# Logit tiles of two PSUM banks, read by one instruction each, in a two-layer hybrid attention kernel

## The chip, the cores and the metric

The kernel runs on one core of one Trainium2 chip. The metric is the device time of one execution in microseconds. Three executions of the kernel before took 3163.4 to 3169.52 us, median 3168.88. The profile shown here is of one more execution.

## The reference

One sequence of 2048 tokens, width 1024, two layers. Each layer projects the normalised state, runs four kinds of attention with four heads of 64 each, gates the joined result and adds the output product to the state:

```python
proj = jnp.einsum('bsd,dc->bsc', h_res, w_in[l])
(fq, fk, fv, f_logit, sq, sk, sv, c_q, c_kv, k_rot, mq, gate) = jnp.split(proj, offsets, axis=-1)
# fox: causal softmax of q.k*scale + f_cum[q] - f_cum[k]
# sb (stick-breaking): w = sigmoid(z) * prod over later valid keys of sigmoid(-z), no softmax
# mla: causal softmax, q and k built from RMS-normed latents c_q, c_kv plus a rope part
# mem: softmax over 256 memory keys
y = jnp.einsum('bsc,cd->bsd', mixed * jax.nn.silu(gate), w_out[l])
h_res = _layer_norm(DEEPNORM_ALPHA * h_res + y, ln_g[l], ln_b[l])
```

All inputs and outputs are float32. The kernel keeps float32 accuracy by splitting operands into a high and a low half in float16 and using three matmuls for one product (`mm3`).

## The kernel before

Work goes in stages, given by `PLAN`: the latents of a layer, then pairs of heads (fox0, fox1, mla0, mla1, sb0, sb1, and both mem pairs together), then the output product. A pair (`pair`) prepares its weights (`wprep`: load, maximum per partition, maximum over partitions in `allmax` through a PSUM tile named pm, scale, split into halves), then goes over four chunks of 512 tokens. For a chunk it makes k, q and v (tiles pk, pq, pv, 24 matmuls each), the gate (pg, `gate_sig` for sb, `gate_tanh` for the others), and then per head and query tile of 128 rows the attention.

`scores` makes the logits of one query tile against up to 1024 keys, in parts of 512 columns, each in its own PSUM tile of one bank. `softmax_tile` (fox, mla) reads each part on DVE: it copies the logits to SBUF, for fox adding the forget sums fb, and takes their maximum (lines 369 and 371); line 376 joins the maxima; ACT then makes the exponentials (line 380). `stick_tile` (sb) reads each part twice on ACT, for sigmoid(-z) and sigmoid(z) (lines 398 and 399); DVE scans the first (401), POOL multiplies (402, 403). In both kinds the weights are split into halves (386, 387, 409, 410), transposed by DMA into tiles named pt, and multiplied with v (858). `half_sum` (449, 450) joins the halves of a head.

PSUM has eight banks. They are given out as four score slots, two slots for the outputs o and two for projections:

```python
ps_s = pool("ps_s", 4, bass.MemoryType.PSUM)
ps_o = pool("ps_o", 2, bass.MemoryType.PSUM)
ps_p = pool("ps_p", 2, bass.MemoryType.PSUM)
```

Score slots also hold the gate (pg), the latent blocks of a layer (pl, read at 537 to 541) and the transposed forget logits (pf, 587), the k and v products of mem, and the tiles of the output product (936, read at 940). Projection slots hold pk, pq, pv, pr and pm. Within a pool slots are handed out in the program's order: a tile takes the slot of the tile before it by the number of slots, once that is free.

The order on each engine is set by a scheduler that goes through the program with a timeline of its own and takes what is ready there, by program order as priority; scores of fox rank 60 places earlier (`SCORE_AHEAD`). Each engine then runs its list in order, and so do the DMA queues: nearly every transfer is issued by SP, in the order of its list. After the latents, `forget` makes running sums of the forget logits, which return through DRAM as fb.

## Time and profile before

| | us |
|---|---|
| median of three executions | 3168.88 |
| lowest, highest | 3163.4, 3169.52 |
| the profiled execution, its own time | 3167.7 |
| span of its profile | 3165.9 |
| PE, DVE, ACT, POOL busy | 2560.0, 2432.3, 1913.7, 1268.3 |
| mean granted TensorE clock | 0.915 of full speed |

Busy time is the union of an engine's instructions. The profile of an instruction runs from its start to the end of its writes; on DVE and ACT the next one starts before that, so the distance of two starts, not the duration, is what an instruction costs in a dense row. An idle stretch of an engine is put down to the instruction whose end released what came next.

### The profile page before, as it was taken

The numbers are of one execution on the slowest core, as the hardware profiler recorded it, in microseconds if no ns is written. First come the engines' busy times: TensorE is split into PE (matmuls) and PEld (weight loads), VectorE is DVE, ScalarE is ACT, GpSimd is POOL, SyncE is SP. The second block draws the span as 40 slices with busy tenths as digits, with TensorE's granted clock in tenths as the row PEclk, the third lists the DMA queues.
The fourth block names the chain that finished last, engine by engine and source line by source line (L and its number), as shares of the span: only waits on it lengthen the run. The fifth ranks groups of instructions, "written<-read, shape, count | busy, mean of one in ns | idle before, by whom it ended". The sixth has DMA issues, their size and how long they took to land. (4 is left out here: it accounts for less than half of the span.)

```text
span 3165.9 us, 47289 instructions
## 1 busy us (share of the span) xinstructions
PE 2560.0 (81%) x16412; PEld 1374.7 (43%) x16412; DVE 2432.3 (77%) x4809; ACT 1913.7 (60%) x3543; POOL 1268.3 (40%) x871
## 2 busy tenths in 40 slices
PE   2589897888886785799978879978888768749898
PEld 2345454444553442444434545544445435325444
DVE  7857867888879989767655575689886998995675
ACT  3447657788757676465235565677776766755600
POOL 5303332333468786432210122233334877771300
PEclk9889899999997897899989999999999889869999
DMA  7747969889845745657845477798987575565652
GB/s 195 195 122 164 197 143 195 174 176 182 169 73 113 155 91 105 150 111 191 234 116 126 105 151 143 159 196 163 186 152 135 89 169 100 101 138 119 163 187 100
DMA packets 1225042, 469.49 MB, mean 148 GB/s; under 512 B 1040305, under 2 KB 1184945, under 8 KB 1224657
## 3 DMA queue, kind: packets, MB, share of 16 engines
q1 hardware_dynamic: 1224800, 466.46, 67.7%
q8 instruction: 129, 2.11, 0.3%
q14 instruction: 113, 0.92, 0.1%
HBM read 141.07 MB, written 50.53 MB: 61 GB/s over the span
## 5 line engine op out<-in xcount | busy, mean ns | idle before, releaser
L387 POOL TENSOR_TENSOR hl<-sb,hl 128x1024 f16<-128x1024 f32 (+2 forms) x192 | 325.0, 1694 | 878.4 <-ACT hl L386 718.5
L858 PE MATMUL o<-pt,v 128*128 128x256 f16 (+3 forms) x3456 | 436.5, 302 | 232.7 <-DMA pt<-hl 232.0
L332 PE MATMUL s<-k,q 128*128 128x512 f16 (+3 forms) x1920 | 523.3, 374 | 120.3 <-DVE sm L369 35.9
L403 POOL TENSOR_TENSOR sg<-sg,kp 128x127 f32<-128x127 f32 (+3 forms) x192 | 396.5, 2068 | 110.4 <-DVE kp L401 80.1
L858 PEld LDWEIGHTS <-v 128*64 128x64 f16 (+1 forms) x3456 | 247.1, 112 | 443.7 <-DMA pt<-hl 226.9
L380 ACT ACTIVATE sb<-sb,sm,sc_all 128x1024 f32<-128x1024 f32 (+7 forms) x384 | 377.4, 983 | 75.8 <-DVE sm L377 75.1
L386 ACT CAST hl<-sb 128x1024 f16<-128x1024 f32 (+7 forms) x384 | 298.4, 790 | 174.7 <-DMA pt<-hl 161.7
L936 PE MATMUL s<-wo,gc 128*128 128x512 f16 x1536 | 335.5, 381 | 2.3 <-DVE yt L940 2.1
L332 PEld LDWEIGHTS <-q 128*128 128x128 f16 x1920 | 184.5, 103 | 309.2 <-issue 193.8
L387 DVE TENSOR_TENSOR hl<-sb,hl 128x1024 f16<-128x1024 f32 (+2 forms) x192 | 208.3, 1085 | 76.4 <-ACT hl L386 75.6
L410 DVE TENSOR_TENSOR hl<-sg,hl 128x128 f16<-128x128 f32 (+3 forms) x192 | 240.5, 1259 | 32.8 <-ACT hl L409 31.7
L409 ACT CAST hl<-sg 128x128 f16<-128x128 f32 (+3 forms) x192 | 152.7, 798 | 178.5 <-DMA pt<-hl 89.4
L369 DVE CUSTOM_DVE_ANT_0 sb<-s,fb 128x512 f32<-128x512 f32 (+2 forms) x320 | 184.2, 604 | 80.9 <-DMA fb<-fds 39.7
L936 PEld LDWEIGHTS <-gc 128*128 128x128 f16 x1536 | 150.9, 98 | 184.5 <-issue 6.2
L398 ACT ACTIVATE kp<-s,sc_all 128x512 f32<-128x512 f32 (+2 forms) x320 | 200.3, 628 | 30.6 <-PE s L332 10.1
L401 DVE TENSOR_TENSOR_SCAN kp<-kp 128x384 f32<-128x384 f32 (+7 forms) x128 | 211.6, 1665 | 6.0 <-ACT kp L398 5.1
L399 ACT ACTIVATE sg<-s,sc_all 128x512 f32<-128x512 f32 (+2 forms) x320 | 200.1, 630 | 25.0 <-DVE hl L410 13.1
L276 PE MATMUL pv<-w,hT 128*128 128x128 f16 x1024 | 191.6, 227 | 18.7 <-DVE k L286 18.7
L276 PE MATMUL pg<-hT,w 128*128 128x512 f16 x512 | 199.8, 390 | 7.6 <-DVE sb L371 6.8
L277 PE MATMUL pg<-hT,w 128*128 128x512 f16 x512 | 199.5, 390 | 0.0
L278 PE MATMUL pg<-hT,w 128*128 128x512 f16 x512 | 198.8, 388 | 0.0
L454 POOL TENSOR_TENSOR og<-og,sg 128x512 f32<-128x512 f32 x64 | 96.4, 1507 | 251.0 <-DVE og L450 176.9
(240 smaller groups left out, 6072.3 us busy)
## 6 DMA issues: line engine op xcount, KB each, us to landing
raw<-in_w_in_dram SPq DMA_DIRECT2D x100, 256.0 KB, 3.6
q<-q SPq DMA_DIRECT2D x128, 128.0 KB, 2.5
fb<-fds SPq DMA_DIRECT2D x32, 512.0 KB, 4.3
gd<-gh SPq DMA_DIRECT2D x128, 128.0 KB, 2.5
raw<-in_w_out_dram SPq DMA_DIRECT2D x64, 256.0 KB, 4.2
gc<-gd SPq DMA_DIRECT2D x64, 256.0 KB, 5.2
yt<-ah SPq DMA_DIRECT2D x32, 512.0 KB, 5.1
raw<-ctd SPq DMA_DIRECT2D x48, 256.0 KB, 3.6
```

Of the source, the lines that this page charges most:

```text
L276: T.matmul(ps, lh, rh, start=(first and k == 0), stop=False)
L332: T.matmul(ps[:, :m], qs[:, h, v, j * P:(j + 1) * P], ks[c][:, h, :m], start=(v == 0), stop=last)
L380: A.activation(t, t, AF.Exp, scale=sc, bias=sm[:, 2:3], accum_out=su[:, b, col:col + 1])
L386: A.copy(hi, t)
L387: (G if j else V).tensor_tensor(lo, t, hi, op=ALU.subtract)
L398: A.activation(keep[:, o:o + m], ps[:, :m], AF.Sigmoid, scale=nsc)
L399: A.activation(w[:, o:o + m], ps[:, :m], AF.Sigmoid, scale=sc)
L401: V.tensor_tensor_scan(keep[:, ::-1], keep[:, ::-1], keep[:, ::-1], cy, op0=ALU.mult, op1=ALU.bypass)
L403: G.tensor_tensor(w[:, :n - 1], w[:, :n - 1], keep[:, 1:n], op=ALU.mult)
L410: V.tensor_tensor(lo, w, hi, op=ALU.subtract)
L858: T.matmul(o[r0:r1, oc + j0 * P:oc + 256], vs[k // 4][:, k % 4, h, 0:r1 - r0], pcol(pt, a, k % 8, kb, j0), start=(n == 1), stop=(n == total))
L936: T.matmul(ps, gc[a][k // 4][:, k % 4, t * P:(t + 1) * P], wo[k][:, b2, n * 512:(n + 1) * 512], start=(k == 0 and a == 0 and b2 == 0), sto ...
```

## The change

Score tiles become two banks wide (two slots of 1024 columns in the same four banks), and every reader takes the whole tile: one DVE read per block of up to 1024 keys in fox and mla, two ACT reads in sb. With up to two maxima left per query tile, their reduction becomes one operation on two numbers, and only where there are two blocks. The first 512 keys of two neighbouring query tiles share one tile (`duo`). The gate, the latent blocks, pf and mem's k and v products move to the projection slots. Mem's logits of a head take one tile instead of two, read by one maximum; the output product's two halves share one tile, read by one instruction.

```diff
-    ps_s = pool("ps_s", 4, bass.MemoryType.PSUM)
+    ps_s = pool("ps_s", 2, bass.MemoryType.PSUM)
...
     def s_tile():
-        return ps_s.tile([P, 512], F32, name=nm("s"), tag="s")
+        return ps_s.tile([P, 1024], F32, name=nm("s"), tag="s")
...
         npass = 3 if kind == "mla" else 2
-        parts = []
+        if n <= 512 and b == 0:
+            if j % 2 == 0:
+                duo[0] = s_tile()
+            full = duo[0][:, (j % 2) * 512:(j % 2) * 512 + n]
+        else:
+            full = s_tile()[:, :n]
         with tc.high_priority(offset=SCORE_AHEAD.get(kind, 0)):
             for o in range(0, n, 512):
                 c, m = 2 * b + o // 512, min(512, n - o)
-                ps = s_tile()
+                ps = full[:, o:o + m]
...
         for b in range(nb):
-            parts, n = scores(kind, h, i, b, qs, ks, qr, kr)
+            ps, n = scores(kind, h, i, b, qs, ks, qr, kr, duo)
             t = granule("sb")[:, :n]
-            for ps, o, m in parts:
-                mx = sm[:, 4 + np_:5 + np_]
-                np_ += 1
-                if kind == "fox":
-                    V.tensor_tensor_reduce(t[:, o:o + m], ps[:, :m], fb[b][:, o:o + m], 1.0, -3.0e38, ALU.add, ALU.max, mx)
-                else:
-                    V.tensor_scalar(t[:, o:o + m], ps[:, :m], 1.0, None, op0=ALU.mult, op1=ALU.max, accum_out=mx)
+            mx = sm[:, 4 + b:5 + b]
+            if kind == "fox":
+                V.tensor_tensor_reduce(t, ps, fb[b][:, :n], 1.0, -3.0e38, ALU.add, ALU.max, mx)
+            else:
+                V.tensor_scalar(t, ps, 1.0, None, op0=ALU.mult, op1=ALU.max, accum_out=mx)
             at.append(t)
         top = sm[:, 4:5]
-        if np_ > 1:
+        if nb > 1:
             top = sm[:, 0:1]
-            V.tensor_reduce(top, sm[:, 4:4 + np_], axis=AX.X, op=ALU.max)
+            V.tensor_tensor(top, sm[:, 4:5], sm[:, 5:6], op=ALU.max)
...
             keep, w = granule("kp")[:, :n], granule("sg")[:, :n]
-            for ps, o, m in parts:
-                A.activation(keep[:, o:o + m], ps[:, :m], AF.Sigmoid, scale=nsc)
-                A.activation(w[:, o:o + m], ps[:, :m], AF.Sigmoid, scale=sc)
+            A.activation(keep, ps, AF.Sigmoid, scale=nsc)
+            A.activation(w, ps, AF.Sigmoid, scale=sc)
...
-        ps = ps_s.tile([P, 512], F32, name=nm("pg"), tag="s")
+        ps = ps_p.tile([P, 512], F32, name=nm("pg"), tag="p")
...
-                    ps = ps_s.tile([P, 512], F32, name=nm("pl"), tag="s")
+                    ps = ps_p.tile([P, 512], F32, name=nm("pl"), tag="p")
...
-                pf = ps_s.tile([P, 512], F32, name=nm("pf"), tag="s")
+                pf = ps_p.tile([P, 512], F32, name=nm("pf"), tag="p")
...
-                ps = ps_s.tile([P, 512], F32, name=nm("pk"), tag="s")
+                ps = ps_p.tile([P, 512], F32, name=nm("pk"), tag="p")
...
-                        pss = [s_tile() for _ in range(2)]
+                        ps = s_tile()
...
-                        for u in range(2):
-                            psv = pss[u].rearrange("p (j k) -> p j k", j=2)
-                            V.tensor_reduce(sm[:, 2 * u:2 * u + 2], psv, axis=AX.X, op=ALU.max)
-                            V.tensor_scalar(sm[:, 4 + 2 * u:6 + 2 * u], sm[:, 2 * u:2 * u + 2], nsc, LN_TOP,
-                                            op0=ALU.mult, op1=ALU.add)
+                        psv = ps.rearrange("p (j k) -> p j k", j=4)
+                        V.tensor_reduce(sm[:, 0:4], psv, axis=AX.X, op=ALU.max)
+                        V.tensor_scalar(sm[:, 4:8], sm[:, 0:4], nsc, LN_TOP, op0=ALU.mult, op1=ALU.add)
...
+                    ps = s_tile()
                     for n in range(2):
-                        ps = s_tile()
...
-                        yv = yt[:, n * 512:(n + 1) * 512]
-                        V.scalar_tensor_tensor(yv, ps, u_o, yv, op0=ALU.mult, op1=ALU.add)
+                    V.scalar_tensor_tensor(yt, ps, u_o, yt, op0=ALU.mult, op1=ALU.add)
```

The scheduler orders the engines anew. Three places follow; in brackets stands the engine whose signal an instruction waits for, by the semaphore's name.

PE in layer 0, where the weight maxima of fox0 (pm_1453) stand. Before, they follow the second latent chunk's pf and the third chunk's first block (pl_1064):

```order
L278 MATMUL pl_888<-w_260,hT_380 128x420
L587 MATMUL pf_973<-id_f,kf_796 4x128 [waits PE_49,Activation_49]
L587 MATMUL pf_973<-id_f,kf_796 4x128 [waits Activation_49]
L137 LDWEIGHTS am_1451 [waits DVE_49]
L137 MATMUL pm_1453<-id_bf,am_1451 2x128
L587 MATMUL pf_973<-id_f,kf_796 4x128 [waits Activation_49] x2
L142 LDWEIGHTS ones_bf
L142 MATMUL pm_1453<-ad_1457,ones_bf 128x2 [waits DVE_49]
L276 LDWEIGHTS hT_742 [waits DMAHW3_49]
L276 MATMUL pl_1064<-w_256,hT_742 128x420 [waits PE_49]
```

Now they come behind the last chunk's last block (pl_1341) and its pf, with fox0's k product (pk_1540) behind them:

```order
L278 MATMUL pl_1341<-w_260,hT_1008 128x420
L588 MATMUL pf_1426<-id_f,kf_1249 4x128 [waits PE_49,Activation_49]
L588 MATMUL pf_1426<-id_f,kf_1249 4x128 x2
L588 MATMUL pf_1426<-id_f,kf_1249 4x128 [waits Activation_49]
L137 LDWEIGHTS am_1451 [waits PE_49,DVE_49]
L137 MATMUL pm_1453<-id_bf,am_1451 2x128 [waits Activation_49]
L142 LDWEIGHTS ones_bf
L142 MATMUL pm_1453<-ad_1457,ones_bf 128x2 [waits DVE_49]
L137 LDWEIGHTS am_1490 [waits DVE_49]
L137 MATMUL pm_1492<-id_bf,am_1490 2x128 [waits Activation_49]
L276 LDWEIGHTS w_1468 [waits Activation_49]
L276 MATMUL pk_1540<-hT_187,w_1468 128x512
```

The weight preparation and the k and q products of fox0 moved from among the latent blocks to behind them.

PE in layer 0's second fox pair, chunk 1, a query tile's scores. Before, the two halves are two tiles (s_4233 and s_4236), and each waits for DVE:

```order
L332 MATMUL s_4233<-k_3629,q_3956 128x512 [waits DVE_49]
L332 LDWEIGHTS q_3956
L332 MATMUL s_4233<-k_3629,q_3956 128x512
L332 LDWEIGHTS q_3956
L332 MATMUL s_4236<-k_3982,q_3956 128x512 [waits DVE_49]
L332 LDWEIGHTS q_3956
L332 MATMUL s_4236<-k_3982,q_3956 128x512
L336 LDWEIGHTS id_bf
L336 MATMUL s_4236<-mask_c,id_bf 128x128
L278 LDWEIGHTS w_3484
```

Now both are one tile (s_4185), with one wait ahead of it:

```order
L337 MATMUL s_4185<-k_3553,q_3876 128x512 [waits DVE_49]
L337 LDWEIGHTS q_3876
L337 MATMUL s_4185<-k_3553,q_3876 128x512
L337 LDWEIGHTS q_3876
L337 MATMUL s_4185<-k_3902,q_3876 128x128
L337 LDWEIGHTS q_3876
L337 MATMUL s_4185<-k_3902,q_3876 128x128
L341 LDWEIGHTS id_bf
L341 MATMUL s_4185<-mask_c,id_bf 128x128
L278 LDWEIGHTS hT_742
```

One wait for DVE stands ahead of all score matmuls of the block instead of one ahead of each half.

ACT in layer 0's sb pairs, the two sigmoids of a block (kp and sg). Before:

```order
L398 ACTIVATE kp_10728<-s_10722,sc_all 128x512 [waits DVE_49,PE_49]
L399 ACTIVATE sg_10729<-s_10722,sc_all 128x512 [waits Pool_49]
L398 ACTIVATE kp_10728<-s_10725,sc_all 128x512 [waits PE_49]
L399 ACTIVATE sg_10729<-s_10725,sc_all 128x512
L398 ACTIVATE kp_10747<-s_10741,sc_all 128x512 [waits DVE_49,PE_49]
L409 CAST hl_10621<-sg_10613 128x1024 [waits DMAHW5_49]
L399 ACTIVATE sg_10748<-s_10741,sc_all 128x512 [waits DVE_49]
```

Now:

```order
L399 ACTIVATE kp_11691<-s_11686,sc_all 128x1024 [waits PE_49]
L400 ACTIVATE sg_11692<-s_11686,sc_all 128x1024
L399 ACTIVATE kp_11707<-s_11702,sc_all 128x1024 [waits PE_49]
L400 ACTIVATE sg_11708<-s_11702,sc_all 128x1024
L459 CAST gh_11636<-og_11242 128x256 [waits DMAHW2_49,Pool_49]
L285 ACTIVATE k_12037<-pk_12012 64x512 [waits PE_49]
L410 CAST hl_11698<-sg_11692 128x1024 [waits DMAHW1_49,Activation_49,Pool_49]
```

Four sigmoids of 512 columns became two of 1024.

## Rows read from the trace of the kernel before

**Rows 1.** The page: busy us (share of the span) and instructions of each engine.

```profile
PE 2560.0 (81%) x16412; PEld 1374.7 (43%) x16412; DVE 2432.3 (77%) x4809; ACT 1913.7 (60%) x3543; POOL 1268.3 (40%) x871
```

**Rows 2.** Busy time by stage: fox, mla, sb, mem of layer 0; fox, mla of layer 1.

```profile
core 0: us, PE busy (x) PEld busy (x) DVE busy (x) ACT busy (x) POOL busy (x), PEclk, DMA share, GB/s
236.00:553.00 317.00, 271.89 (x1993) 154.46 (x1992) 239.50 (x676) 219.85 (x392) 101.43 (x68) 0.95 0.83 174
553.00:861.00 308.00, 261.65 (x1703) 140.95 (x1701) 259.61 (x693) 237.80 (x415) 110.29 (x75) 0.94 0.89 178
861.00:1336.00 475.00, 351.24 (x2414) 195.20 (x2412) 420.57 (x447) 301.43 (x529) 332.60 (x219) 0.85 0.56 115
1336.00:1468.00 132.00, 122.33 (x612) 58.64 (x611) 81.02 (x143) 91.32 (x216) 36.94 (x28) 0.96 0.63 146
1761.00:2097.00 336.00, 289.36 (x2132) 163.85 (x2132) 230.40 (x652) 218.99 (x391) 95.35 (x66) 0.94 0.75 153
2097.00:2410.00 313.00, 258.49 (x1690) 138.13 (x1689) 265.01 (x689) 236.06 (x413) 109.10 (x74) 0.95 0.88 171
```

**Rows 3.** Waits at score matmuls, fox and mla, layers 0 and 1: us, times.

```profile
  DVE sm L369: 20.4, 13
  DVE sb L371: 12.9, 17
...
  DVE sb L369: 10.7, 7
...
  DVE sb L371: 16.3, 15
  DVE sm L369: 15.9, 16
...
  DVE sb L369: 23.0, 9
```

**Rows 4.** The page's costliest groups: fox's maximum, sb's first sigmoid.

```profile
L369 DVE CUSTOM_DVE_ANT_0 sb<-s,fb 128x512 f32<-128x512 f32 (+2 forms) x320 | 184.2, 604 | 80.9 <-DMA fb<-fds 39.7
...
L398 ACT ACTIVATE kp<-s,sc_all 128x512 f32<-128x512 f32 (+2 forms) x320 | 200.3, 628 | 30.6 <-PE s L332 10.1
```

**Rows 5.** Timeline of DVE in fox: start us, us, instruction.

```profile
340.84 0.67 DVE L369 CUSTOM_DVE_ANT_0 sb<-s,fb 128x512 f32<-128x512 f32 x1
...
341.45 0.27 DVE L369 CUSTOM_DVE_ANT_0 sb<-s,fb 128x128 f32<-128x128 f32 x1
...
341.66 0.67 DVE L128 TENSOR_REDUCE wm<-raw 128x1 f32<-128x512 f32 x1
```

**Rows 6.** Timeline of ACT in sb.

```profile
2718.73 0.68 ACT L399 ACTIVATE sg<-s,sc_all 128x512 f32<-128x512 f32 x1
2719.30 0.37 ACT L398 ACTIVATE kp<-s,sc_all 128x128 f32<-128x128 f32 x1
2719.55 0.38 ACT L399 ACTIVATE sg<-s,sc_all 128x128 f32<-128x128 f32 x1
```

**Rows 7.** Waits of DVE in layer 0's sb: us, times, longest us.

```profile
DVE hl L410 <- ACT hl L409: 16.5, 16, 3.0
DVE og L450 <- ACT og L449: 9.9, 4, 4.6
```

**Rows 8.** Timeline: last latent block, first fox maximum, in layer 0, in layer 1.

```profile
182.28 0.46 ACT L537 COPY craw<-pl 128x384 f32<-128x384 f32 x1
...
235.81 0.29 DVE L369 CUSTOM_DVE_ANT_0 sb<-s,fb 128x128 f32<-128x128 f32 x1 [5.80 <-DMA fb<-fds]
...
1707.27 0.48 ACT L537 COPY craw<-pl 128x384 f32<-128x384 f32 x1 [2.73 <-PE pl L278]
...
1760.97 0.29 DVE L369 CUSTOM_DVE_ANT_0 sb<-s,fb 128x128 f32<-128x128 f32 x1 [5.12 <-DMA fb<-fds]
```

**Rows 9.** Groups by form: mem's maxima and the products behind them.

```profile
L805 DVE TENSOR_REDUCE smm<-s 128x2 f32<-128x512 f32 x64 | 43.2, 686 | 19.6 <-PE s L801 19.1
...
L806 DVE TENSOR_SCALAR smm<-smm,sc_all 128x2 f32<-128x2 f32 x64 | 20.9, 337 | 0.6
```

More of the change, by code (lines that the diff above doesn't have):

```diff
@@ L315, in s_tile, with scores @@
     def s_tile():
-        return ps_s.tile([P, 512], F32, name=nm("s"), tag="s")
-    def scores(kind, h, i, b, qs, ks, qr, kr):
+        return ps_s.tile([P, 1024], F32, name=nm("s"), tag="s")
+    def scores(kind, h, i, b, qs, ks, qr, kr, duo):
         n = min(1024, (i + 1) * P - 1024 * b)
@@ L336, in scores @@
                     T.matmul(ps[:, m - P:m], id_bf, masks["s" if kind == "sb" else "c"], start=False, stop=True)
-                parts.append((ps, o, m))
-        return parts, n
+        return full, n
     def pcol(pt, a, k, kb, j0):
@@ L354, in emit_T, with softmax_tile @@
         dmaT(pt[:, 16 * j:16 * j + 2 * (n // P), :], both)
-    def softmax_tile(kind, h, i, j, qs, ks, qr, kr, fb, sc, nsc, su):
+    def softmax_tile(kind, h, i, j, qs, ks, qr, kr, fb, sc, nsc, su, duo):
         sm = smp.tile([P, 8], F32, name=nm("sm"), tag="sm", bufs=12)
@@ L389, in softmax_tile, with stick_tile @@
         return half
-    def stick_tile(h, i, j, qs, ks, sc, nsc):
+    def stick_tile(h, i, j, qs, ks, sc, nsc, duo):
         carry = [None]
         def half(b, pt):
-            parts, n = scores("sb", h, i, b, qs, ks, None, None)
+            ps, n = scores("sb", h, i, b, qs, ks, None, None, duo)
             keep, w = granule("kp")[:, :n], granule("sg")[:, :n]
-            for ps, o, m in parts:
-                A.activation(keep[:, o:o + m], ps[:, :m], AF.Sigmoid, scale=nsc)
-                A.activation(w[:, o:o + m], ps[:, :m], AF.Sigmoid, scale=sc)
+            A.activation(keep, ps, AF.Sigmoid, scale=nsc)
+            A.activation(w, ps, AF.Sigmoid, scale=sc)
             cy = TOP if carry[0] is None else carry[0]
@@ L423, in gate_tanh @@
     def gate_tanh(w, u2, c, hops_c):
-        ps = ps_s.tile([P, 512], F32, name=nm("pg"), tag="s")
+        ps = ps_p.tile([P, 512], F32, name=nm("pg"), tag="p")
         mm3(ps, wops(w), hops_c)
@@ L750, in pair @@
                 vm = vp.tile([P, 4, 2, P], F16, name=nm("v"), tag="v")
-                ps = ps_s.tile([P, 512], F32, name=nm("pv"), tag="s")
+                ps = ps_p.tile([P, 512], F32, name=nm("pv"), tag="p")
                 for t in range(2):
@@ L797, in pair @@
                         pe = granule("pe", (P, 4, MEM))
-                        pss = [s_tile() for _ in range(2)]
+                        ps = s_tile()
                         for j in range(4):
                             for v in range(2):
-                                T.matmul(pss[j // 2][:, (j % 2) * 256:(j % 2 + 1) * 256],
-                                         qs[:, h, v, j * P:(j + 1) * P], km[:, h, :MEM], start=(v == 0), stop=(v == 1))
-                        for u in range(2):
-                            psv = pss[u].rearrange("p (j k) -> p j k", j=2)
-                            V.tensor_reduce(sm[:, 2 * u:2 * u + 2], psv, axis=AX.X, op=ALU.max)
-                            V.tensor_scalar(sm[:, 4 + 2 * u:6 + 2 * u], sm[:, 2 * u:2 * u + 2], nsc, LN_TOP,
-                                            op0=ALU.mult, op1=ALU.add)
-                            for j in range(2 * u, 2 * u + 2):
-                                A.activation(pe[:, j], psv[:, j % 2], AF.Exp, scale=sc, bias=sm[:, 4 + j:5 + j],
-                                             accum_out=su[:, 0, h * 4 + j:h * 4 + j + 1])
+                                T.matmul(ps[:, j * MEM:(j + 1) * MEM], qs[:, h, v, j * P:(j + 1) * P], km[:, h, :MEM], start=(v == 0), stop=(v == 1))
+                        psv = ps.rearrange("p (j k) -> p j k", j=4)
+                        V.tensor_reduce(sm[:, 0:4], psv, axis=AX.X, op=ALU.max)
+                        V.tensor_scalar(sm[:, 4:8], sm[:, 0:4], nsc, LN_TOP, op0=ALU.mult, op1=ALU.add)
+                        for j in range(4):
+                            A.activation(pe[:, j], psv[:, j], AF.Exp, scale=sc, bias=sm[:, 4 + j:5 + j],
+                                         accum_out=su[:, 0, h * 4 + j:h * 4 + j + 1])
                         hl = phl.tile([P, 2, 4, MEM], F16, name=nm("hl"), tag="phl")
@@ L829, in pair @@
                         nb = (2 * g + 1) // 8 + 1
-                        halves = []
+                        halves, duo = [], [None]
                         for j in range(2):
@@ L833, in pair @@
                             if kind == "sb":
-                                halves.append(stick_tile(h, i, j, qs, ks, sc, nsc))
+                                halves.append(stick_tile(h, i, j, qs, ks, sc, nsc, duo))
                             else:
-                                halves.append(softmax_tile(kind, h, i, j, qs, ks, qr, kr, fb, sc, nsc, su))
+                                halves.append(softmax_tile(kind, h, i, j, qs, ks, qr, kr, fb, sc, nsc, su, duo))
                         nk = 2 * g + 2
```

4 lines of the change are left out of this document (2 added, 2 removed).

## The prediction

> **What bounds the kernel now.** I read the busy shares first. Over the whole program TensorE (PE) is busy 81%, VectorE (DVE) 77% and ScalarE (ACT) 60% [rows 1]: no engine is full, so the average says nothing about a single wait. Next comes the table by stage [rows 2]. In layer 0 the fox pairs fill 236 to 553 us, the mla pairs 553 to 861, the sb pairs 861 to 1336, mem 1336 to 1468; in layer 1 fox runs from 1761 to 2097 and mla to 2410. In fox PE is the fullest (271.89 of 317 us, 86%; DVE 76%). In mla PE (85%), DVE (84%) and the DMA engines (89%) are level. In sb DVE is busy 420.57 of 475 us, 89%, ACT only 63%. In mem PE is busy 122 of 132 us. So a microsecond of DVE work saved in fox and mla is worth a part of a microsecond, one of ACT work in sb less, and one of either in mem nearly nothing.
>
> Third I read who stops whom at the score tiles [rows 3]. In fox and mla of layer 0 PE stood 20.4 + 12.9 us, 13 + 17 times, in front of a score matmul until DVE had read an earlier score tile; in layer 1 16.3 + 15.9 us, 15 + 16 times. The other way round the fox maximum on DVE stood 10.7 and 23.0 us for scores. Together: 61 stops of PE, 65.5 us; 33.7 us of DVE. This is what the change of tiles and of banks can touch.
>
> **Part 1: fewer, longer reads on DVE (fox and mla).** A head has 16 query tiles; they take 40 blocks of at most 512 keys and 24 of at most 1024. With four fox and four mla heads in two layers, 640 reads (320 in fox [rows 4], as many in mla) become 384, so 256 go. What one costs is read from starts, not from durations, since neighbours overlap: a 512-wide read starts at 340.84 and its accumulator read and the next block at 341.45, 0.61 us on; the 128-wide one frees DVE after 0.21 us [rows 5]. That is 1.04 ns a column and 0.077 us fixed. 256 x 0.077 = 19.7 us. The small reduction over the partial maxima becomes an operation on two numbers and is left out for 64 tiles of 512 to 1024 keys; at the same fixed 0.077 us that is 4.9 us more. So DVE loses about 25 us of work in four stages that take 1274 us. If all of it counted: -25; if PE and the transposes cover it: 0. DVE is 68 to 85% busy there, next to a PE at 83 to 86%, so I take half: **-12**.
>
> The Trainium skill (Perfetto Trace Analysis, Optimizing Scalar/DVE Operations) gives an overhead of about 125 ns for a DVE operation on PSUM; by that 256 reads are worth 32 us, not 19.7. The rows measure 0.077 us, and the sum goes by the rows.
>
> **Part 2: two score tiles of two banks in place of four of one, and the gate out of them.** Two effects of opposite sign. A gate product held one of four score slots from its first matmul to the end of its evacuation; now it takes a projection slot, and scores can go on beside it. At best that ends all starving of DVE for scores in fox: -34 us (10.7 + 23.0). Against it, a score tile is now free only when all 1024 columns are read, one 512-read (0.61 us) later than its first half was, and DVE can't begin before the second half is written. If each of the 61 stops of PE gets longer by that: +37 us. What waits behind a score matmul on PE are the projections and the probability-times-value products, and behind these the half sums on ACT and DVE. No row decides between the two; the middle is **0**, with both ends kept.
>
> **Part 3: sigmoids of 1024 columns on ACT (sb).** Two reads per block: 2 x 320 [rows 4] become 2 x 192, 256 fewer. A 512-wide sigmoid lets the next start after 0.57 us (2718.73 to 2719.30), a 128-wide one after 0.25 us [rows 6]: 0.83 ns a column, 0.143 us fixed. 256 x 0.143 = 37 us of ACT in two stages of some 470 us. But ACT is not what is full there. DVE's idle time behind ACT in layer 0's sb is 16.5 us (the low-half subtraction behind its cast) and 9.9 us (the half sums) [rows 7]. The scan can also begin sooner, after the first of two long sigmoids rather than the third of four. I take a fifth of those 26 us, 5 a layer: **-10**, between 0 and -37.
>
> The same section of the Trainium skill puts the overhead of a ScalarE operation on PSUM at about 51 ns; that would make 13 us of these 37. The rows show 0.143 us from start to start.
>
> **Part 4: latent products and pf in the projection banks, and what that does to the order at the first fox pair.** This is the one place where the order changes in kind. The weight maxima of the next pair (pm) use the projection slots, and slots are handed out in program order. Before, the latents sat in the score slots, so fox0's pm, weights and k and q products ran between the latent blocks of layer 0. Now they come after the last pf. In layer 1 the kernel before already has just that order, so layer 1 shows what layer 0 will look like. The time from the last latent block to the first fox maximum is the same in both: 182.28 to 235.81 and 1707.27 to 1760.97, 53.5 and 53.7 us [rows 8]; it ends with the landing of the forget sums (fb), so losing the head start costs nothing there. It costs afterwards: layer 1's fox stage takes 336 us against 317, with 17.5 us more of PE work in it [rows 2]. So up to +19. Part of it comes back, since the input norm no longer shares DVE, ACT and PE with fox0's weights and products; how much no row shows. I take two thirds: **+13**, between 0 and +19.
>
> In the other stages the gate's and mem's products only queue in two slots instead of six. Outside mla each product is 24 matmuls long, and while one is made its neighbour is evacuated; I put it at nothing. If that cover fails, pk of the next chunk is late, and its scores with it.
>
> **Part 5: mem and the output product.** Mem: 64 maxima of 0.686 us become 32 of twice the width, 32 x 0.077 = 2.5 us, and 64 small products of 0.337 us become 32, 10.8 us [rows 9]. All of it lies beside a PE that is 93% busy: **-2**, at most -13. Output: one evacuation of 1024 columns starts when the second half is written; PE hides that except behind the last tile of a layer, 512 x 1.04 ns = 0.53 us, twice: **+1**.
>
> **Sum.** -12 + 0 - 10 + 13 - 2 + 1 = -10 us. The profiled execution took 3167.7 us (span 3165.9 and 1.8 around it), 1.2 below the median of the three runs, 3168.88. Forecast: **3158 us**. A measurement of this kernel can tell about 0.2% (6 us) from no change.
>
> **Rivals.**
> - *Coarser tiles stall PE (slower).* The place is the score matmul at PE's queue head, the price 0.61 us at each of 61 stops, +37; with the head start lost (+13), half of parts 1 and 3 (-11) and +1 that is +40: 3208 us. It decides once the stops of PE behind score reads grow from 65.5 us to over some 88 (by the 22 that parts 1 and 3 bring). For it: DVE and ACT are not full, yet PE waits for them 61 times. Against: four halves and two wholes are equally many columns ahead. The Trainium skill has this rule too, in the section named above: where Scalar or Vector aren't saturated but cause bubbles on other engines, breaking up instructions may let work be completed sooner. By it this rival would hold; the 61 stops are such bubbles, and no row here shows a longer read. Chance 0.2.
> - *The relief is covered.* PE at 86% and DMA at 83 to 89% pace fox and mla, DVE paces sb, and parts 1 and 3 give nothing: +13 + 1, 3182 us, or near no change if the norm gives the head start back. Chance 0.2.
> - *All of it counts.* Full part 1 (-25), half the starving gone (-17), 26 us of waits behind ACT gone in sb (-26), half of mem (-7), +13 + 1: 3107 us. For it: scores and gate no longer wait for each other, and every stage has several engines near 85% held up by one another. Chance 0.18.
> - That the merge doesn't happen is excluded: the compiled order holds 192 reads of each kind.
>
> **Chances and range.** The forecast has 0.42, with 3140 to 3170 as its own range. A quarter of it and a third of the second rival fall within 0.2%. Faster: 0.32 + 0.18 = 0.50. Same: 0.10 + 0.07 = 0.17. Slower: 0.13 + 0.20 = 0.33. For 8 in 10 the range must reach both outer rivals: 3100 to 3205.
>
> **What would show it.** Right: 192 DVE reads of each kind with 1.15 us between starts at 1024 columns; ACT busy in each sb stage down by some 18 us with DVE's hardly changed; layer 0's fox stage with PE work like layer 1's; the first fox maximum some 53 us after the last latent block in both layers. Wrong: PE's stops behind score reads above 88 us (first rival), stages of the old length at lower DVE and ACT busy time (second), or fox and mla shorter by over 10 us each (third). The forecast is most exposed in parts 2 and 4, where the rows only bound.

## The result and the profile after

The changed kernel takes 3277.5 us, the kernel before 3167.6 beside it on the same chip: ratio 1.0351, 95% interval 1.0336 to 1.0367. That is 110 us slower where 10 faster were forecast, and 72 above the top of the range.

The page of the changed kernel, busy time of each engine over a span of 3277.4 us, against [rows 1]:

```profile
PE 2560.7 (78%) x16412; PEld 1378.2 (42%) x16412; DVE 2412.0 (74%) x4137; ACT 1880.9 (57%) x3287; POOL 1262.2 (39%) x871
```

TensorE does the same work (2560.7 against 2560.0 us), DVE 20 us less, ACT 33 less. The span grew by 111.5 us. So the whole loss is time in which PE stood still, and no engine became fuller.

The table by stage of the changed kernel (fox, mla, sb and mem of layer 0, fox, mla and sb of layer 1; columns as in [rows 2]):

```profile
230.00:576.00 346.00, 291.73 (x2166) 164.93 (x2165) 246.09 (x532) 221.80 (x394) 99.85 (x68) 0.96 0.76 159
576.00:901.00 325.00, 267.20 (x1693) 141.19 (x1693) 260.10 (x550) 238.86 (x417) 108.84 (x74) 0.92 0.84 166
901.00:1391.00 490.00, 352.00 (x2436) 199.16 (x2435) 421.56 (x446) 283.20 (x403) 334.59 (x221) 0.84 0.57 114
1391.00:1531.00 140.00, 119.03 (x584) 55.81 (x583) 81.88 (x130) 94.61 (x221) 37.72 (x31) 0.94 0.61 139
...
1833.00:2171.00 338.00, 293.71 (x2163) 168.11 (x2161) 231.94 (x504) 215.81 (x388) 90.28 (x65) 0.95 0.73 150
2171.00:2485.00 314.00, 258.18 (x1732) 140.37 (x1730) 255.76 (x550) 240.21 (x420) 109.35 (x75) 0.96 0.88 172
2485.00:2974.00 489.00, 344.12 (x2409) 194.45 (x2408) 418.83 (x445) 284.19 (x401) 336.15 (x220) 0.85 0.56 114
```

Against [rows 2]: layer 0's fox is 29 us longer, with 20 us more PE work in it, its mla 17, its sb 15. ACT's busy time in sb fell from 301.43 to 283.20 us with DVE's unchanged, as forecast, and the stage still got longer.

The reads themselves came out as forecast. First the changed kernel's groups for fox's maximum and sb's first sigmoid, then those of mem's bias and maximum (count, least, median and greatest ns, first and last start), then DVE's timeline late in layer 0's fox stage:

```profile
L371 DVE CUSTOM_DVE_ANT_0 sb<-s,fb 128x1024 f32<-128x1024 f32 (+2 forms) x192 | 170.5, 908 | 78.7 <-DMA fb<-fds 42.0 <-PE s L337 18.1 <-PE s L341 13.3
...
L399 ACT ACTIVATE kp<-s,sc_all 128x128 f32<-128x128 f32 (+3 forms) x192 | 165.7, 863 | 38.8 <-PE s L341 16.3 <-PE s L337 14.8 <-DVE hl L411 6.5
```

```profile
L805 DVE TENSOR_SCALAR smm<-smm,sc_all x32: 212/229/1215, 1390.2 to 3086.8; 128x4 f32<-128x4 f32 x32
...
L804 DVE TENSOR_REDUCE smm<-s x32: 1209/1224/1226, 1388.0 to 3082.9; 128x4 f32<-128x1024 f32 x32
```

```profile
565.56 1.22 DVE L371 CUSTOM_DVE_ANT_0 sb<-s,fb 128x1024 f32<-128x1024 f32 x1
...
566.70 0.44 DVE L378 TENSOR_TENSOR sm<-sm 128x1 f32<-128x1 f32 x1
```

192 reads stand in the place of 320 [rows 4], and a 1024-wide one frees DVE after 1.14 us (565.56 to 566.70; 1.15 was forecast from [rows 5]).

Waits at the score tiles of the changed kernel, fox and mla, first layer 0, then layer 1 (us, times), to set against [rows 3]:

```profile
  DVE sm L371: 24.2, 20
  DVE sb L373: 21.9, 16
```

```profile
  DVE sb L373: 20.8, 17
...
  DVE sm L371: 14.8, 12
...
  PE s L337: 9.9, 4
```

That is 65 stops of PE and 81.7 us, against 61 and 65.5: sixteen microseconds more, of 110. The fox maximum's own waits for scores hardly fell. Behind the key product they went from 23.0 to 9.9 us in layer 1 (the last row), but now the last matmul before a read is more often the one that adds the mask (L336 before, L341 after). Over both layers the two together were 33.7 + 3.6 us before (the group's row below) and are 18.1 + 13.3 now (row L371 above): 37.3 against 31.4.

```profile
L369 DVE CUSTOM_DVE_ANT_0 sb<-s,fb 128x512 f32<-128x512 f32 (+2 forms) x320 | 184.2, 604 | 80.9 <-DMA fb<-fds 39.7 <-PE s L332 33.7 <-PE s L336 3.6
```

Last latent block and first fox maximum, layer 0 and layer 1, against [rows 8]:

```profile
179.19 0.48 ACT L538 COPY craw<-pl 128x384 f32<-128x384 f32 x1 [0.56 <-PE pl L278]
...
230.07 0.29 DVE L371 CUSTOM_DVE_ANT_0 sb<-s,fb 128x128 f32<-128x128 f32 x1 [2.89 <-DMA fb<-fds]
...
1781.60 0.48 ACT L538 COPY craw<-pl 128x384 f32<-128x384 f32 x1 [2.73 <-PE pl L278]
...
1833.06 0.29 DVE L371 CUSTOM_DVE_ANT_0 sb<-s,fb 128x128 f32<-128x128 f32 x1 [2.78 <-DMA fb<-fds]
```

50.9 and 51.5 us, where some 53 were forecast, and fox starts 5.7 us earlier than before. The loss comes behind this point.

What grew elsewhere, PE's waits over the whole run, shows part of it. Before and after (us, times, longest):

```profile
PE pm L137 <- DVE am L135: 81.7, 11, 30.6
...
PE s L332 <- ACT sg L399: 25.0, 22, 4.0
...
PE pv L276 <- DVE k L286: 18.7, 12, 3.8
```

```profile
PE pm L137 <- DVE am L135: 140.8, 13, 30.9
PE s L337 <- ACT sg L400: 46.7, 22, 6.5
...
PE pv L276 <- DVE k L286: 30.3, 12, 7.5
...
PE pg L276 <- DVE q L286: 7.5, 3, 5.3
```

"pv behind k" is the value product that waits until the key product's slot is evacuated, "pg behind q" the gate product behind the query product. The last one isn't in the list of before: there the gate had a score slot. The wait of pm, the weight maxima, grew most, by 59.1 us, but it misleads. In the latent stage of layer 0 (40 us to the first fox maximum) it is 41.0 us now and 2.5 before, and yet fox starts earlier, so these 38.5 us cost nothing by themselves. In sb, the wait behind the second sigmoid grew by 21.7 us; the read that PE waits for now covers the whole two-bank tile (with the reads cut, below, it is back at 25.2, and the kernel no faster).

Stage times of four kernels, from the first score read of a stage to the first of the next (mem from the loading of its exponential's function table, just before the first exponential, to its last), in us. "After, reads cut" is the run after_split below:

| stage | before | after | moved products alone | after, reads cut |
|---|---|---|---|---|
| fox, layers 0 and 1 | 317.0, 335.5 | 346.5, 338.5 | 346.9, 345.4 | 355.4, 338.6 |
| mla | 308.3, 313.7 | 325.0, 313.2 | 310.3, 319.8 | 316.2, 326.5 |
| sb | 474.2, 468.3 | 488.9, 487.6 | 490.3, 489.5 | 481.7, 476.3 |
| of sb, from the start of its last first sigmoid to mem's table load | 45.5, 45.4 | 59.3, 61.9 | 58.8, 58.3 | 52.4, 51.8 |
| mem | 111.2, 110.4 | 120.6, 122.7 | 112.9, 111.9 | 122.9, 123.2 |

### The profile page after: what moved, and what is told of

Its sections match the earlier page's. It is cut to its first block, busy times and chain, and to the rows that moved or that the text cites. A ratio compares the mean times of both kernels' runs of the same rounds, so it can differ in the third digit from the quotient of the medians.

```text
span 3277.4 us, 46250 instructions
## 1 busy us (share of the span) xinstructions
PE 2560.7 (78%) x16412; PEld 1378.2 (42%) x16412; DVE 2412.0 (74%) x4137; ACT 1880.9 (57%) x3287; POOL 1262.2 (39%) x871
## 5 line engine op out<-in xcount | busy, mean ns | idle before, releaser
L337 PE MATMUL s<-k,q 128*128 128x512 f16 (+3 forms) x1920 | 513.4, 377 | 141.9 <-ACT sg L400 46.7
L856 PE MATMUL o<-pt,v 128*128 128x256 f16 (+3 forms) x3456 | 422.3, 295 | 232.3 <-DMA pt<-hl 232.0
L404 POOL TENSOR_TENSOR sg<-sg,kp 128x127 f32<-128x127 f32 (+4 forms) x192 | 373.8, 1948 | 104.5 <-DVE kp L402 87.3
L411 DVE TENSOR_TENSOR hl<-sg,hl 128x128 f16<-128x128 f32 (+3 forms) x192 | 253.1, 1326 | 52.8 <-ACT hl L410 52.2
L371 DVE CUSTOM_DVE_ANT_0 sb<-s,fb 128x1024 f32<-128x1024 f32 (+2 forms) x192 | 170.5, 908 | 78.7 <-DMA fb<-fds 42.0
L276 PE MATMUL pv<-w,hT 128*128 128x128 f16 x1024 | 195.5, 230 | 30.3 <-DVE k L286 30.3
L277 PE MATMUL pv<-w,hT 128*128 128x128 f16 x1024 | 195.2, 229 | 0.0
L373 DVE TENSOR_SCALAR_CACHE_REDUCE sb<-s 128x1024 f32<-128x1024 f32 (+2 forms) x192 | 172.0, 907 | 31.3 <-PE s L339 17.3
L278 PE MATMUL pv<-w,hT 128*128 128x128 f16 x1024 | 194.9, 229 | 0.0
```

The lines of the kernel that those rows point to most:

```text
L276: T.matmul(ps, lh, rh, start=(first and k == 0), stop=False)
L277: T.matmul(ps, lh, rl, start=False, stop=False)
L278: T.matmul(ps, ll, rh, start=False, stop=(last and k == n - 1))
L337: T.matmul(ps[:, :m], qs[:, h, v, j * P:(j + 1) * P], ks[c][:, h, :m], start=(v == 0), stop=last)
L404: G.tensor_tensor(w[:, :n - 1], w[:, :n - 1], keep[:, 1:n], op=ALU.mult)
L411: V.tensor_tensor(lo, w, hi, op=ALU.subtract)
```

## The experiments

Each is given with its ratio to the kernel before and the 95% interval; a per cent is 31.7 us.

**Each half of the change alone.** First only the moved products, the tiles as before (reloc_only):

```diff
-        ps = ps_s.tile([P, 512], F32, name=nm("pg"), tag="s")
+        ps = ps_p.tile([P, 512], F32, name=nm("pg"), tag="p")
...
-                    ps = ps_s.tile([P, 512], F32, name=nm("pl"), tag="s")
+                    ps = ps_p.tile([P, 512], F32, name=nm("pl"), tag="p")
...
-                ps = ps_s.tile([P, 512], F32, name=nm("pk"), tag="s")
+                ps = ps_p.tile([P, 512], F32, name=nm("pk"), tag="p")
```

(and so for pf and mem's pv.)

> Score tiles of one bank as before; only the gate, the latent blocks with pf, and mem's k and v products move to the projection slots. Theory P (the two crowded projection slots are the cost): 3240 to 3290 us, with the stage starts of the changed kernel (fox of layer 0 some 30 us longer than before, mem some 15 us per layer). Theory T (the two-bank score tiles are the cost): 3165 to 3185 us, only layer 0's fox longer, by up to 19 us.

Measured: 3248.4 us, 1.0246 (1.0230 to 1.0261). PE's waits there:

```profile
PE pv L276 <- DVE k L286: 32.9, 13, 7.8
...
PE pg L276 <- DVE q L286: 18.3, 11, 7.0
```

The two waits of the changed kernel are here without its tiles. Then the tiles and long reads alone, with gate, latents and mem's products each in one half of a two-bank score tile (tiles_only):

```diff
-        ps = ps_p.tile([P, 512], F32, name=nm("pg"), tag="p")
+        ps = ps_s.tile([P, 1024], F32, name=nm("pg"), tag="s")[:, :512]
```

(and so for the others.)

> Score tiles of two banks, each read by one instruction, as in the change; the gate, the latent blocks with pf, and mem's k and v products stay in score slots (each takes half of one of the two). Theory P: 3135 to 3175 us, the relief of DVE and ACT being what is left. Theory T: 3240 to 3300 us; the more so as a gate or latent block now holds one of two slots instead of one of four.

Measured: 3241.8 us, 1.0228 (1.0211 to 1.0245). Both halves cost, 79 and 72 us, so each theory that put the whole cost on one half fell. Together they cost 110, less than the sum; one reason may be that this second run also lends out half of all score space for each product, which no run separates. Layer 1's fox was 313.8 us there, 22 shorter than before, layer 0's 319.0; why only the one got shorter is open.

**The moved products one by one** (gate_only, lat_only with pf, mem_only: the first, second and third line pair of the diff above).

> The kernel before, with only the gate product moved to the projection slots. Theory P with the gate as the crowding product: 3200 to 3260 us, every pair longer, and the gaps from pair to pair with them. Theory P with the latents and mem as the crowding ones: 3160 to 3175 us. Theory T: 3150 to 3175 us.

> The kernel before, with only the latent blocks and pf moved to the projection slots. If the lost head start of layer 0's first fox pair is worth what the recorded text took: 3175 to 3190 us. If it is the larger part of the change's loss: 3200 to 3230 us, all of it ahead of layer 0's mla. Layer 1 unchanged within 5 us, as its order is the same.

> The kernel before with only mem's key and value products moved from score slots to projection slots. Gate alone cost 39 us, the latents alone 43, all three together 79; if the parts add up, mem's are worth nothing: within 6 us of before, 3163 to 3175, mem at 106 to 109 us in both layers. Rival (parts overlap, and mem's share is hidden in that): 10 us or more above before, with a longer gap between sb and mem.

Gate alone: 3208.3 us, 1.0126 (1.0109 to 1.0143). Latents alone: 3212.6, 1.0134 (1.0118 to 1.0149). Mem alone: 3192.3, 1.0102 (1.0082 to 1.0121). So 39, 43 and 31 us, and 79 together: my subtraction that left nothing for mem was wrong, the parts overlap. Waits of PE with the gate alone moved:

```profile
PE pv L276 <- DVE k L286: 26.4, 13, 5.3
...
PE pg L276 <- DVE q L286: 14.6, 11, 5.3
```

The latents alone made layer 0's fox 329.9 us, the 13 us more that part 4 of the prediction gave it. But mla grew too, by 17 and 21 us, against the expectation; in layer 1's mla (2120.6 to 2455.5 us there) PE was busy 272.3 us at a granted clock of 0.89, against 259.2 at 0.95 in the same stage of the kernel before. So PE's busy time grew by 13 us of the 21, at a lower clock. What leads from the latents to there is not settled.

Mem alone shows the queue plainly. Mem's value and query products between sb and mem in layer 0 (first and last start, us), in the kernel before, where the last of sb's first sigmoids starts at 1289.8:

```profile
L278 PE MATMUL pv<-w,memT x32: 219/219/219, 1303.1 to 1328.1; 128*128 128x128 f16 x32
...
L278 PE MATMUL pq<-hT,w x23: 379/379/389, 1313.6 to 1339.2; 128*128 128x512 f16 x23
```

and with mem's products moved, where it starts at 1283.7:

```profile
L278 PE MATMUL pv<-w,memT x32: 217/219/219, 1297.2 to 1328.9; 128*128 128x128 f16 x32
...
L278 PE MATMUL pq<-hT,w x28: 379/379/379, 1330.2 to 1349.5; 128*128 128x512 f16 x28
```

Before, the query product ran among the value products, 24 us behind that sigmoid. Moved, pk and pv hold both projection slots, and the first query product starts once the value products are done, 47 us behind it. The first exponential of mem, with its table load, is late too: 62.1 us behind the same sigmoid against 45.5, and 64.8 against 45.4 in layer 1. The changed kernel has this gap as well (table above).

**Is the kernel before just lucky in its order?** Any edit reorders instructions. One redundant small operation per pair (16 more DVE operations by the profile) in the kernel before (null_pair) and in the changed one (after_null), and another look-ahead for fox's scores in each (ahead64, after_ahead40):

```diff
             V.tensor_scalar(nsc, sc, -1.0, None, op0=ALU.mult)
+            V.tensor_scalar(nsc, sc, -1.0, None, op0=ALU.mult)
...
-SCORE_AHEAD = {"fox": 60}
+SCORE_AHEAD = {"fox": 64}
```

> The kernel before, with one operation on a single column (the sign of a pair's scale) done twice: 14 extra operations of 0.2 us, 3 us in all. It changes nothing else but the scheduler's order (about a tenth of PE's rows stand elsewhere). Theory N (the order before is a lucky one, and any disturbance of it costs): 3190 to 3215 us. Theories P and T (placement, tile width): 3165 to 3178 us.

> The kernel before, with fox's scores ranked 64 places earlier instead of 60: the same work in another order, on a fifth of PE's rows. Theory N: 3185 to 3215 us, with stages that the edit doesn't touch (mla, sb, mem) longer too. Theories P and T: 3160 to 3180 us.

> The changed kernel with the same doubled operation per pair. Theory N: it moves by 15 us or more either way, 3240 to 3300 us. Theories P and T: within 10 us of the changed kernel, 3270 to 3290 us.

> The changed kernel with fox's scores ranked 40 places earlier instead of 60, since a score block now counts fewer instructions. Theory N: another draw, 3230 to 3300 us, mla, sb and mem changing with it. Theory P: 3265 to 3290 us, as the projection slots are as crowded. Theory T: fox alone changes, by up to 15 us.

Measured: null_pair 1.0010 (1.0000 to 1.0021), ahead64 1.0015 (1.0004 to 1.0027), after_null 1.0307 (1.0285 to 1.0328), after_ahead40 1.0303 (1.0287 to 1.0318). Reordering is worth some 3 to 15 us, not 110. It is also the size below which a difference between two edited kernels proves little here.

**Long reads or wide slots?** The changed kernel, every tile read in two instructions of 512 again (after_split), and only mem's and the output's reads cut (after_mo):

```diff
-            mx = sm[:, 4 + b:5 + b]
+            for o in range(0, n, 512):
+                m = min(512, n - o)
...
-            A.activation(keep, ps, AF.Sigmoid, scale=nsc)
+                A.activation(keep[:, o:o + m], ps[:, o:o + m], AF.Sigmoid, scale=nsc)
```

> The changed kernel with its tiles of two banks and its moved products, but every tile read in two instructions of 512 columns as before (fox and mla maxima, sb sigmoids, mem maxima, output evacuation). It differs from the run that only moved products (3248 us) by the width of a slot alone, and from the changed kernel (3268 to 3278) by the length of a read alone. Theory R (the long reads cost the last 20 to 30 us: a half is finished only when the whole is): 3240 to 3256. Rival S (the slot of two banks costs them: it is handed out again only when both halves are read): 3265 to 3285, whatever the reads.

> The changed kernel with only the reads of mem (maxima and their bias) and of the output product cut in two again; fox, mla and sb keep the long reads. Mem takes 114 and 116 us in the changed kernel against 107 and 107 before, the output stage some 7 us more than before in each layer. Theory R2 (those two merged reads lengthen mem and output, since there PE is full and nothing else is in flight): 25 to 30 us come back, 3245 to 3255, with mem at 105 to 108 us and output at 202 and 171. Rival (these stages are longer through the slots or the moved products): 3268 to 3280.

Measured: 3281.5 us, 1.0374 (1.0357 to 1.0392), and 3289.9, 1.0402 (1.0381 to 1.0423). Both expectations that blamed the reads fell: cut, the kernel is no faster. But the nearly equal totals hold two differences of opposite sign. Layer 1's exponentials of mem, with the products moved alone, in the changed kernel, and with every read cut:

```profile
L809 ACT ACTIVATE pe<-s,smm,sc_all x64: 547/559/565, 2965.3 to 3075.4; 128x256 f32<-128x256 f32 x64
```

```profile
L807 ACT ACTIVATE pe<-s,smm,sc_all x64: 548/559/567, 2973.7 to 3094.7; 128x256 f32<-128x256 f32 x64
```

```profile
L813 ACT ACTIVATE pe<-s,smm,sc_all x64: 551/556/566, 2961.3 to 3082.8; 128x256 f32<-128x256 f32 x64
```

Up to the last exponential the version with cut reads is 12 us ahead of the changed kernel. Behind it little but the output product is left; from there to the end of the span it takes 196.5 us, against 182.7 in the changed kernel and 172.9 with the products moved alone. In that stretch PE waits for the cut reads of output tiles (us, times, longest), and in the changed kernel for none:

```profile
PE s L940 <- DVE yt L943: 12.8, 14, 6.5
```

The longest of these stops goes back to a transfer (yt) for which DVE itself waited 5.4 us. The 12 and the 14 us are of the size that reordering has, so these runs give the length of a read no price.

What differs between after_split and the moved products alone is the slot: 1.0374 against 1.0246, 40 us. Some 24 of it stand in that last stretch (196.5 against 172.9), where the changed kernel loses 10. Mem shows another part. Its 64 exponentials of layer 0 (first and last start) with four one-bank slots (before), then with two two-bank slots (after):

```profile
L809 ACT ACTIVATE pe<-s,smm,sc_all x64: 547/559/582, 1336.5 to 1446.0; 128x256 f32<-128x256 f32 x64
```

```profile
L807 ACT ACTIVATE pe<-s,smm,sc_all x64: 548/559/570, 1391.8 to 1510.6; 128x256 f32<-128x256 f32 x64
```

109.5 and 118.8 us; with the reads cut 121.1, with the products moved and four slots 111.2.

**Slots counted out.** The numbers of score, accumulator and projection slots are 4, 2 and 2 before. The kernel before with 3, 2, 2 (a bank left empty) and with 3, 2, 3, and the moved products with 3, 2, 3:

```diff
-    ps_s = pool("ps_s", 4, bass.MemoryType.PSUM)
+    ps_s = pool("ps_s", 3, bass.MemoryType.PSUM)
...
-    ps_p = pool("ps_p", 2, bass.MemoryType.PSUM)
+    ps_p = pool("ps_p", 3, bass.MemoryType.PSUM)
```

> The kernel before with three score slots in place of four, one bank of PSUM left empty and nothing moved. It prices one score slot, so that the next two runs can be read. Theory Q (projection slots are the scarce ones, scores have room): 3170 to 3200. Rival S (scores need their four slots: PE's stops behind score reads, 65 us before, double or more): 3220 or more.

> The kernel before with three score slots and three projection slots, nothing moved. Theory Q (a third projection slot is worth something already before the change): 5 to 30 us under the run with three and two slots. Rival (two projection slots are enough as long as gate and latents stay out): within 5 us of it.

> The kernel that only moved products (3248 us with four score slots and two projection slots), with three and three. Theory Q (the moved products cost 79 us because they queue in two slots): against the run of before with three and three the cost falls to 40 us or less. Rival F (they cost by the place in the order of slots that the program gives them, a late gate or latent block holding up what comes after it, however many slots there are): it stays at 60 to 90 us above that run.

Measured: 3266.4 us, 1.0328 (1.0311 to 1.0345); 3232.4, 1.0228 (1.0213 to 1.0243); 3212.4, 1.0166 (1.0151 to 1.0181). The fourth score slot is worth 105 us (the kernel before took 3161.1 beside it), well beyond the bound that the rival was given. The rival's condition was not met: PE's stops behind score reads did not double. With three score slots, busy times and PE's waits:

```profile
PE 2596.6 (79%) x16412; PEld 1385.6 (42%) x16412; DVE 2444.5 (75%) x4809; ACT 1923.4 (59%) x3545; POOL 1241.6 (38%) x871
```

```profile
PE o L858 <- DMA pt<-hl: 272.0, 126, 10.5
...
PE s L332 <- DVE sb L371: 38.0, 37, 4.0
PE s L332 <- DVE sm L369: 38.0, 35, 3.4
```

The stops behind score reads are 76.0 us, against 64.8 in the same view of the kernel before. The span is 103 us longer: PE's busy time grew by 37 us for the same matmuls (2596.6 against 2560.0) at a granted clock of 0.901 against 0.915, and PE's waits for transposed weights (pt) grew from 232.0 to 272.0 us. So the price of a slot stands mostly elsewhere than at the tiles that use it.

A third projection slot is worth 34. And with three of each the same moved products that cost 79 us gain 20. Waits of PE there:

```profile
PE pg L276 <- DVE k L286: 1.2, 2, 0.7
```

In this run the gate waits 1.2 us for a slot, and the value product's wait behind k is gone from the list; in the run with the products moved and two slots they were 18.3 and 32.9. One caution: with three score slots, taking gate and latents out of them may also be worth more than with four. No run has the moved products with three score and two projection slots, so how much of the swing of 99 us is the projection slots' is not shown.

Mem again seems to count slots. Layer 0's exponentials with three score slots (before_32), then with five (before_512, which has one accumulator, below):

```profile
L809 ACT ACTIVATE pe<-s,smm,sc_all x64: 544/558/566, 1382.6 to 1502.4; 128x256 f32<-128x256 f32 x64
```

```profile
L809 ACT ACTIVATE pe<-s,smm,sc_all x64: 547/559/567, 1359.2 to 1461.1; 128x256 f32<-128x256 f32 x64
```

119.8 us with three, 109.5 with four, 101.9 with five; two slots of two banks, 118.8, took about as long as three of one. But the count does not settle it alone. With four slots and only the gate moved (gate_only) layer 0's exponentials took 116.3 us, and layer 1's 118.5:

```profile
L809 ACT ACTIVATE pe<-s,smm,sc_all x64: 546/560/570, 1349.8 to 1466.1; 128x256 f32<-128x256 f32 x64
```

**A product that holds its slot long.** The weight maxima (pm) moved from the projection to the score slots, with the other products moved (reloc_pm) and in the kernel before (before_pm):

```diff
-        ps = ps_p.tile([P, 512], F32, name=nm("pm"), tag="p")
+        ps = ps_s.tile([P, 512], F32, name=nm("pm"), tag="s")
```

> The kernel that only moved products (3248 us), with the small products of the weight maxima (pm) moved out of the projection slots into the score slots. Theory P (the moved products make the next pair's weight maxima wait in two slots, and with them the next pair's start): at least half of the 79 us comes back, 3210 or less, layer 0's fox stage at 330 us or less. Rival Q (the products of one chunk, k, q, v and gate, wait for each other's evacuation in the two slots): 3240 to 3256.

> The kernel before with one thing moved, the small products of the weight maxima (pm) from the two projection slots into the four score slots. Theory P2 (two projection slots are the scarce ones already before the change, 81.7 us of stops of PE in front of pm): faster than before by 5 to 25 us, 3145 to 3164. Rival (a score slot lent out is as dear as a projection slot gained, since scores wait for it): 3169 to 3190.

Measured: 3355.5 us, 1.0607 (1.0589 to 1.0625), and 3346.4, 1.0577 (1.0555 to 1.0599). Both theories fell, by 100 us and more. The pm of the first mla pair, in the kernel before, whose last fox read ends at 544.7, and then with pm moved, where it ends at 551.0:

```profile
L137 PE MATMUL pm<-id_bf,am x2: 217/217/217, 497.7 to 501.7; 128*2 128x128 bf16 x1, 128*1 128x128 bf16 x1
```

```profile
L137 PE MATMUL pm<-id_bf,am x2: 216/216/217, 548.9 to 549.5; 128*2 128x128 bf16 x1, 128*1 128x128 bf16 x1
```

Slots go out in the order in which the program asks. In a pool of scores, the next pair's maxima are asked for behind all scores of this pair. They then run at its end instead of 43 us ahead of it, and the weights and first products of the next pair come after them: from the last fox read to the first mla read it takes 36 us instead of 8. A shared pool thus costs an order as well as a slot. So these two runs don't tell whether pm and gate disturb each other in the projection slots; that wasn't separated.

**Can the banks be had elsewhere?** One accumulator in place of two pays for a third projection slot beside four score slots, with the products moved (reloc_413), or for a fifth score slot with nothing moved (before_512):

```diff
-    ps_o = pool("ps_o", 2, bass.MemoryType.PSUM)
+    ps_o = pool("ps_o", 1, bass.MemoryType.PSUM)
```

> The moved products with four score slots and three projection slots, the bank taken from the two accumulators of the probability-times-value products, of which one is left. A third projection slot turned the moved products from 79 us of cost into a gain of 20 (three score slots), and a fourth score slot is worth 103 us in the kernel before. If the second accumulator is cheap (under 40 us), this beats both kernels: 3150 or less. Rival (with one accumulator each head's first value product waits at the head of PE's queue for the half sum of the head before): 3190 or more.

> The kernel before with five score slots, one accumulator and two projection slots, nothing moved. The third score slot was worth 70 us or more beyond two; if a fifth still helps and the second accumulator is cheap: 3155 or less. Rival (the second accumulator is worth more than a fifth score slot): 3175 or more.

(The premise in the second, the third score slot's worth, was measured by no run; only the fourth's was.) Measured: 3257.5 us, 1.0267 (1.0246 to 1.0288), and 3211.9, 1.0129 (1.0114 to 1.0144). The first value product of a head now waits for the half sum of the one before. Both rivals held: the second accumulator is worth more than the bank gives elsewhere. PE's waits in the first and in the second:

```profile
PE o L858 <- DVE og L450: 68.0, 17, 8.4
```

```profile
PE o L858 <- DVE og L450: 50.1, 17, 7.6
```

No division of the eight banks that was run beats the kernel before.

## Why the prediction was wrong

The step that failed is the last paragraph of part 4: "In the other stages the gate's and mem's products only queue in two slots instead of six [...] I put it at nothing." Moved alone, the gate costs 39 us and mem's products 31, and with the latents' 43 the three cost 79. Its exposure was written beside it ("if that cover fails, pk of the next chunk is late"). What the traces show late is the value product behind the key's evacuation, the gate behind the query's, and mem's query product behind mem's own key and value products. The cover was priced by the length of a product on PE (24 matmuls; the value product is 96 shorter ones, about as long), not by the time its slot stays taken until ACT and DVE have emptied it.

Point by point:

- **Part 1, -12, and part 3, -10.** The reads went, by the counts and times given. Of the 22 us nothing can be told from zero: the changed kernel and its version with cut reads differ by 0.23% with intervals that overlap, less than reordering alone did in the changed kernel, and the 12 us by which the cut version is ahead at the last exponential point the other way. In sb 18 and 17 us of ACT work went in the two layers; DVE's waits behind ACT, the 26 us of [rows 7], did not fall:

```profile
DVE hl L411 <- ACT hl L410: 25.1, 21, 3.0
...
DVE og L451 <- ACT og L450: 8.8, 5, 3.4
```

  They are 33.9 us now. So the length of the sigmoids did not set the low-half subtraction's wait. Idle time of DVE behind ACT was counted as if any ACT saving would shorten it.
- **Part 2, 0 between -34 and +37.** The wide tiles add 31 us to the moved products (110 against 79), with cut reads 40: near the bad end or beyond it, but by another way than the bound, so that the end comes out near is luck. Stops at score tiles in fox and mla rose by 16 us only [rows 3]; the 61 stops times 0.61 us were the wrong place to look. The starving that was to end, 37.3 us, is still 31.4. Of the 31 us between the spans of after_split and of the moved products alone, mem has 21, where part 5 gave -2, and the stretch behind the last exponential 24, with 12.8 of stops behind output reads in it; the other stretches change their sign and sum to -14. "Four halves and two wholes are equally many columns ahead" was the argument against; in mem, two wholes took as long as three halves, but what else lengthens mem (gate_only) was not separated.
- **Part 4's first term, +13.** The place was right. With the latents alone, layer 0's fox took 13 us more. That is the stage's loss, not the price of the move: the whole run lost 43, as both mla stages grew. In the changed kernel it took 29 more, the gate's queue on top (+14 alone).
- **Part 5.** Mem's maxima and bias operations became half as many, as counted [rows 9]; the stage became longer by part 2.
- **The rivals.** The first, that coarser tiles stall PE, was right in its sign and in naming granularity; its condition, stops over 88 us in fox and mla, was not met (81.7), and its 3208 us lacks the projection queue. The second was right in that no relief shows in the total. No rival had the moved products as its mechanism, though the change moves five of them into a pool of two slots.

The Trainium skill (Perfetto Trace Analysis, Optimizing Scalar/DVE Operations) says that where Scalar or Vector aren't saturated but cause bubbles on other engines, breaking up instructions may let work be completed sooner. The run with every read cut in two shows no gain from it in the whole time: 1.0374 against 1.0351. What moved the time far more was how many slots there were to be handed out: 105 us for one of four.

What stays open: how the 79 us divide among the queue in the slots and the order in which the moved products are handed their slots, why the wide tiles cost what they do outside fox and mla's score stops, why mla grew when the latents alone were moved, and why the parts of the change add up to more than the whole.

## What to carry to other kernels

Before moving a product into another PSUM pool, write down for each stage who else holds its slots, from the first matmul to the end of the evacuation, and in which order the program asks for them; the busy shares, 81% at most here, did not show it. Price a slot by a run that takes one away: here one of four score slots was worth 105 us, while all the stops that the trace names at score tiles in fox and mla were 65. Such a price is the whole run's, with the new order and PE's clock in it. Merging reads saved busy time here (20 us of DVE, 33 of ACT), but the coarser slots that it took cost more idle time on PE than it gave back.

## What was not expected of the hardware

- One of four score banks is worth 105 us (1.0328), a third projection bank 34 us beside three of score, a second accumulator more than a fifth score bank. The division of PSUM's eight banks moved the time by more than the 20 us of DVE work and 33 of ACT work that the change took away.
- Mem's exponentials took 119.8, 109.5 and 101.9 us with three, four and five score slots, at the same length of each (558 or 559 ns); with four slots and the gate moved they took 116.3, so the number of slots is not all of it.
- A few microseconds of weight maxima, handed a slot of another pool, cost 183 us. The order shows in the trace, 36 us in place of 8 between fox and mla in layer 0; PE itself was busy 53 us longer (2612.8 us) at a granted clock of 0.899.
